# Three attention heads of a group transposed in one unit, their value products in the unit behind

## The chip, the cores and the metric

The kernel runs on one core of a Trainium2 chip. The metric is the device time of one execution in microseconds (us). Before the change it is 906.09 us, the median of three runs that lie between 906.04 and 906.09 us.

The engines of the core are named as in the profile. PE is TensorE, which multiplies matrices and writes its results to PSUM; PEld is its loading of weights, which runs beside the multiplying. DVE is VectorE, ACT is ScalarE, POOL is GpSimd, and SP issues most of the transfers. Each engine works through its own list of instructions in order, and an instruction can wait until another engine has counted up to a given number of instructions.

## The reference

One layer of an encoder, for 256 tokens of width 2048, all in fp32. What matters here is the attention group: 12 query heads of 128 columns share 4 heads of keys and values, so that three query heads belong to one group of keys.

```python
h = _rmsnorm(x, norm1_g)
proj = h @ w_in                      # q | k | v | u
scores = jnp.einsum('bnqkgd,bnskd->bnkgqs', qb, kb) * (HEAD_DIM ** -0.5) + alibi
p = jnp.exp(scores - m)
p = p / (jnp.sum(p, axis=-1, keepdims=True) + jnp.exp(sink_b - m))
out = jnp.einsum('bnkgqs,bnskd->bnqkgd', p.astype(v.dtype), vb)
f = jnp.real(jnp.fft.fft2(ug, axes=(1, 3), norm='ortho'))   # then a linear map per group
a, f = _rmsnorm(attention, attn_out_g), _rmsnorm(fourier, fourier_out_g)
x = x + jnp.concatenate([a, f], axis=-1) @ w_out
x = x + _conv_ffn(_rmsnorm(x, norm2_g), w_up, dw_w, dw_b, w_down)
```

A final RMSNorm follows. The attention and the Fourier group are each normed over their own width, so the kernel needs a sum of squares per token for each of the two.

## The kernel before

Weights come from memory in pieces of 1 MB. ACT and DVE split each piece into a high and a low part (`parts`, lines 185 and 186), and PE multiplies with both parts. The work of PE on one piece is a *unit*. Units 8 to 23 compute the projections of 4 key heads and 12 query heads, in the order k, q, q, q for each group; head 0 is unit 9, head 1 unit 10, head 2 unit 11, head 3 unit 13, and so on up to head 11 in unit 23. Units 24 to 39 are the output projection, and the feed-forward part follows.

A unit of a projection is 16 pairs of matmuls, one of 128x512 with the high part (line 394) and one of 128x256 with the low part (line 396). The attention work of the heads is laid between the units, by a table of what is done how many units after the unit of a head: the scores (line 662) two units later, the exponentials behind them (line 692), the division by the sum (`weigh`, line 705) three units later, the transposing of the weights on PE four units later (`turn`, four 128x128 transposes, line 712, read out by `turn_out`: ACT writes the high part `pt0`, line 724, DVE the low part `pt1`, line 725), the product with the values five units later (`values`, six matmuls, line 734, read out by `values_out`: ACT squares, line 491, and writes the high part of `cat`, line 234, DVE its low part, line 235). The squares of each head are added up by POOL (line 496) into `sq_a`. `total` (line 503) sums them over the partitions with matmuls that have a column of ones.

Each unit `i` runs in four steps, which fix the order of each engine's list: the list `before` (PE work of the heads), then the unit's own matmuls, then `beside` (reading out on ACT and DVE), then the split of the weights for unit `i + 2`, then `behind`.

```python
    def unit(i, work):
        run(before, i)
        work(*halves.pop(i))
        run(beside, i)
        step(i)
        run(behind, i)
```

The buffers that matter are eight PSUM banks, four in the pool `mm` (the projections, `ps_k` and `ps_q`, and most value products, `ps_o`) and four in `dn` (scores `ps_s`, transposes `ps_t`, sums `ps_totf` and `ps_tota`, the last value products), three buffers for `parts`, and four for `sc`, the attention weights. A new tile takes a buffer that has come free; where none is free its first writer waits for the reader that gives one up. The tile that collects a head's squares (`sq1`) has one buffer.

Of the kernel before, what the change touches and what calls it, by code (L numbers as in the profile page):

```python
# [9 lines left out]
F32R = mybir.dt.float32r  # L10
# [3 lines left out]
P = 128  # L14
# [6 lines left out]
GQA = 3  # L21
NG = 4
AW = NH * HD
FW = NG * P
# [27 lines left out]
N_OUT = N_QK + len(QK_ORDER)  # L52
# [44 lines left out]
def block_kernel(  # L97
# [24 lines left out]
    mm = ctx.enter_context(tc.tile_pool(name="mm", bufs=4, space=bass.MemoryType.PSUM))  # L122
    dn = ctx.enter_context(tc.tile_pool(name="dn", bufs=4, space=bass.MemoryType.PSUM))

    def f32(ap):
        return ap.bitcast(F32)
# [182 lines left out]
    ph = pa.enter_context(tc.tile_pool(name="pa", bufs=1))  # L309
# [103 lines left out]
    before, beside, behind = {}, {}, {}  # L413

    def at(when, i, f, *a):
        when.setdefault(i, []).append((f, a))
# [190 lines left out]
    def fourier_channels_steps():  # L607
        for g in range(NG):
            i = 9 + g
            at(beside, i, fourier_channels_copy, g)  # L610
            at(beside, i + 1, fourier_channels_join, g)
            at(behind, i + 1, fourier_channels_out, g)
        at(beside, 15, total_scale, "f", FW)


    ps_v = [bank(mm, f"ps_v{b}") for b in range(2)]
# [15 lines left out]
    def qk_out(kind, h, ps):  # L632
        tmp = ph.tile([P, S], F32, tag="tmp", name=f"tmp_{kind}{h}", bufs=2)
        nc.scalar.activation(tmp, ps[:, S : 2 * S], AF.Copy)
        add = ph.tile([P, S], F32, tag="add", name=f"add_{kind}{h}", bufs=2)
        nc.vector.tensor_tensor(add, ps[:, 0:S], tmp, ALU.add)
        if kind == "k":
            nc.vector.tensor_tensor(add, add, r1b, ALU.mult)
        st["add", kind, h] = add
# [77 lines left out]

    def turn_out(h):
        ps = st.pop(("t", h))
        pt = [  # L720
            ph.tile([P, 512], F32R, tag=f"pt{q}", name=f"pt{q}{h}", bufs=2)
            for q in range(2)
        ]
        nc.scalar.activation(pt[0], ps, AF.Copy)
        nc.vector.tensor_tensor(pt[1], ps, f32(pt[0]), ALU.subtract)
        st["p", h] = pt
# [20 lines left out]
    slot_of = {kh: N_QK + n for n, kh in enumerate(QK_ORDER)}  # L747
    for i in range(N_QK, N_OUT + 8):
        heads = {i - s: h for (kind, h), s in slot_of.items() if kind == "q"}
        new = [kh for kh, s in slot_of.items() if i - s == 1]  # L750
        if i - 9 in range(NG):
            at(before, i, fourier_channels, i - 9)
        if 5 in heads:
            at(before, i, values, heads[5], mm if i < N_OUT else dn)
        if 4 in heads:
            at(before, i, turn, heads[4])
        if i == 15:
            at(before, i, total, sq_f, "f")
        if 2 in heads:
            at(before, i, scores, heads[2])  # L760

        for kind, h in new:
            if kind == "q":
                at(beside, i, lambda k=kind, h=h: qk_out(k, h, st.pop(("ps", k, h))))
        if 4 in heads:
            at(beside, i, turn_out, heads[4])
        if 3 in heads:
            at(beside, i, weigh, heads[3])
        for kind, h in new:
            if kind == "k":  # L770
                at(beside, i, lambda k=kind, h=h: qk_out(k, h, st.pop(("ps", k, h))))
            at(beside, i, qk_parts, kind, h)
        if 2 in heads:
            at(beside, i, scores_out, heads[2])
            at(behind, i, exps, heads[2])
        if 5 in heads:
            at(beside, i, values_out, heads[5])

    fourier_channels_steps()
    for n, (kind, h) in enumerate(QK_ORDER):  # L780

# [56 lines left out]
    for n, (c, kq) in enumerate(OUT_ORDER):  # L838
        i = N_OUT + n
# [391 lines left out]
    i = up_index[n]  # L1231
# [156 lines left out]
```

## Time and profile before

| what | value |
|---|---|
| median of three runs | 906.09 us |
| the profiled execution: its own time | 906.14 us |
| span from first to last instruction | 904.4 us |
| granted TensorE clock, mean | 0.998 |
| PE, matmuls | 895.6 us busy, 99% |
| PEld, weight loads | 811.1 us, 90% |
| DVE | 745.1 us, 82% |
| ACT | 547.2 us, 61% |
| POOL | 51.7 us, 6% |

The profile comes from one execution, and its sums are made against that execution: its time of 906.14 us is 1.74 us more than its span, and 0.05 us above the median. A timeline row gives start and length of an instruction, or of some in a run (x4), then engine, line, output<-inputs; in brackets stands how long the engine stood idle before it and for whom. The stated length of a matmul holds its passage through the array, so matmuls overlap in the rows: what a matmul costs is read from start to start. The stretch that the change touches lies between 80 and 190 us of the span.

### The profile page before, as it was taken

The numbers are of one execution on the slowest core, as the hardware profiler recorded it, in microseconds if no ns is written. First come the engines' busy times: TensorE is split into PE (matmuls) and PEld (weight loads), VectorE is DVE, ScalarE is ACT, GpSimd is POOL, SyncE is SP. The second block draws the span as 40 slices with busy tenths as digits, with TensorE's granted clock in tenths as the row PEclk, the third lists the DMA queues.
The fourth block names the chain that finished last, engine by engine and source line by source line (L and its number), as shares of the span: only waits on it lengthen the run. The fifth ranks groups of instructions, "written<-read, shape, count | busy, mean of one in ns | idle before, by whom it ended". The sixth has DMA issues, their size and how long they took to land.

```text
span 904.4 us, 12754 instructions
## 1 busy us (share of the span) xinstructions
PE 895.6 (99%) x5073; PEld 811.1 (90%) x5073; DVE 745.1 (82%) x892; ACT 547.2 (61%) x663; POOL 51.7 (6%) x65
## 2 busy tenths in 40 slices
PE   9999999999999999999999999999999999999996
PEld 8899999888899999999999999999999999999885
DVE  7579888666668877889887998878988789998996
ACT  7767677555454656556565565566655566656544
POOL 0001111000000000000000000000000000000004
PEclk9999999999999999999999999999999999999999
DMA  9864544456568678677898779887787988779652
GB/s 365 332 234 145 187 152 175 146 180 226 192 231 283 231 242 251 188 257 230 275 266 271 245 258 287 258 276 237 275 250 245 312 263 262 242 240 286 217 196 94
DMA packets 32908, 214.86 MB, mean 238 GB/s; under 512 B 3632, under 2 KB 4016, under 8 KB 8528
## 3 DMA queue, kind: packets, MB, share of 16 engines
q1 hardware_dynamic: 28448, 183.89, 54.5%
q0 software_dynamic: 4112, 29.49, 17.1%
q8 instruction: 40, 0.66, 0.3%
q10 hardware_dynamic: 288, 0.66, 0.2%
q14 instruction: 20, 0.16, 0.0%
HBM read 211.93 MB, written 2.10 MB: 237 GB/s over the span
## 4 chain that ended last, share of the span: by engine, by line
PE 95%; DVE 2%; POOL 1%; issue 1%; ACT 0%; POOLq 0%; ACTq 0%; DVEq 0%
PE ps_val L394 17%; PE ps_gate L394 17%; PE ps_gate L396 8%; PE ps_val L396 8%; PE ps_q L394 5%; PE ps_P L1105 3%; PE ps_P L1107 3%; PE ps_P L1106 3%; PE ps_N L1105 2%; PE ps_N L1107 2%; PE ps_N L1106 2%; PE ps_u L286 2%; PE ps_q L396 2%; PE ps_a L377 2%; PE ps_a L379 2%; PE ps_a L378 2%
## 5 line engine op out<-in xcount | busy, mean ns | idle before, releaser
L186 DVE TENSOR_TENSOR parts<-raw,parts 128x2048 fp32r<-128x2048 f32 (+1 forms) x129 | 293.2, 2273 | 49.4 <-ACT parts L185 48.9
L185 ACT ACTIVATE parts<-raw 128x2048 fp32r<-128x2048 f32 (+1 forms) x129 | 245.4, 1902 | 46.7 <-PE ps_a L379 12.4
L394 PE MATMUL ps_val<-hU,parts 128*128 128x512 f32 x688 | 227.7, 382 | 0.0
L394 PE MATMUL ps_gate<-hU,parts 128*128 128x512 f32 x688 | 227.3, 382 | 0.0
L396 PE MATMUL ps_val<-hU,parts 128*128 128x256 f32 x688 | 187.5, 273 | 0.0
L396 PE MATMUL ps_gate<-hU,parts 128*128 128x256 f32 x688 | 186.9, 273 | 0.0
L394 PEld LDWEIGHTS ps_val<-hU,parts 128*128 128x128 f32 x688 | 130.0, 189 | 18.1
L394 PEld LDWEIGHTS ps_gate<-hU,parts 128*128 128x128 f32 x688 | 130.0, 189 | 18.1
L396 PEld LDWEIGHTS ps_val<-hU,parts 128*128 128x128 f32 x688 | 132.0, 192 | 0.8
L396 PEld LDWEIGHTS ps_gate<-hU,parts 128*128 128x128 f32 x688 | 131.8, 192 | 0.9
L883 ACT ACTIVATE ft_g<-ps_gate 128x256 f32<-128x256 f32 x43 | 16.5, 384 | 112.7 <-PE ps_gate L396 110.0
L394 PE MATMUL ps_q<-hT,parts 128*128 128x512 f32 x192 | 62.6, 384 | 0.0
L883 ACT ACTIVATE ft_v<-ps_val 128x256 f32<-128x256 f32 x43 | 16.5, 384 | 73.4 <-PE ps_val L396 73.4
L1105 PE MATMUL ps_P<-parts_P,op_P 128*128 128x512 f32 x144 | 54.7, 380 | 0.0
L1106 PE MATMUL ps_P<-parts_P,op_P 128*128 128x512 f32 x144 | 54.6, 379 | 0.0
L1107 PE MATMUL ps_P<-parts_P,op_P 128*128 128x512 f32 x144 | 54.6, 379 | 0.0
L396 PE MATMUL ps_q<-hT,parts 128*128 128x256 f32 x192 | 50.4, 273 | 0.0
L991 DVE TENSOR_TENSOR parts_N<-sumw,parts_N 128x2048 fp32r<-128x2048 f32 x18 | 41.2, 2289 | 9.9 <-ACT parts_N L990 9.9
L1105 PE MATMUL ps_N<-parts_N,op_N 128*128 128x512 f32 x108 | 41.0, 380 | 0.0
L1106 PE MATMUL ps_N<-parts_N,op_N 128*128 128x512 f32 x108 | 40.9, 379 | 0.0
L1107 PE MATMUL ps_N<-parts_N,op_N 128*128 128x512 f32 x108 | 40.9, 379 | 0.0
L394 PEld LDWEIGHTS ps_q<-hT,parts 128*128 128x128 f32 x192 | 36.1, 189 | 4.7
(346 smaller groups left out, 1557.7 us busy)
## 6 DMA issues: line engine op xcount, KB each, us to landing
raw<-in_w_up SPq DMA_DIRECT2D x86, 1024.0 KB, 6.2
raw<-in_w_in SPq DMA_DIRECT2D x20, 1024.0 KB, 5.0
sumw<-in_w_down POOLq DMA_DIRECT2D x18, 1024.0 KB, 8.5
raw<-in_w_out SPq DMA_DIRECT2D x16, 1024.0 KB, 4.8
raw<-in_w_down_late SPq DMA_DIRECT2D x4, 1024.0 KB, 5.8
u_raw<-in_u_in SPq DMA_DIRECT2D x4, 768.0 KB, 9.3
raw<-in_w_down_last SPq DMA_DIRECT2D x4, 768.0 KB, 4.2
u_raw<-in_u_in SPq DMA_DIRECT2D x6, 384.0 KB, 6.3
```

The costliest lines, as they stand in the source:

```text
L185: nc.scalar.activation(hi, raw, AF.Copy)
L186: nc.vector.tensor_tensor(lo, raw, f32(hi), ALU.subtract)
L286: nc.tensor.matmul(ps_u[b], block(hk(k), part, b, True), in_turn(w), start=k == 0 and n == 0, stop=k == NK - 1 and n == 2,)
L377: nc.tensor.matmul(ps, ah, wh, start=first and q == q0, stop=False)
L378: nc.tensor.matmul(ps, al, wh, start=False, stop=False)
L394: nc.tensor.matmul(ps, hi[:, s], in_turn(h), start=k == 0, stop=False)
L396: nc.tensor.matmul(ps[:, 0:S], lo[:, s], in_turn(h)[:, 0:P], start=False, stop=k == NK - 1)
L883: nc.scalar.activation(tmp, ps[:, S : 2 * S], AF.Copy)
L991: nc.vector.tensor_tensor(lo, src, f32(hi), ALU.subtract)
L1105: nc.tensor.matmul(ps, o[:, 0, p, :], wh, start=first and p == 0, stop=False)
L1106: nc.tensor.matmul(ps, o[:, 1, p, :], wh, start=False, stop=False)
L1107: nc.tensor.matmul(ps, o[:, 0, p, :], wl, start=False, stop=end)
```

## The change

The transposes of the three heads of a group move together into one unit, four units after the last of the three; the first head's transposes move by two units and the second's by one. The three value products follow together in the next unit. The value product of the middle head takes its PSUM bank from `dn`, the two others from `mm`; from unit 24 on all are in `dn`, as before. `pt0` has three buffers in place of two. `pt1` has no buffers of its own any more and takes one of the four `sc` buffers. The sum over partitions of the Fourier squares, and what follows from it, move from unit 15 to unit 19. No arithmetic changes, and every instruction of before is there.

```diff
@@ fourier_channels_steps
-        at(beside, 15, total_scale, "f", FW)
+        at(beside, 19, total_scale, "f", FW)
@@ turn_out
         pt = [
-            ph.tile([P, 512], F32R, tag=f"pt{q}", name=f"pt{q}{h}", bufs=2)
-            for q in range(2)
+            ph.tile([P, 512], F32R, tag=tag, name=f"pt{q}{h}", bufs=bufs)
+            for q, (tag, bufs) in enumerate([("pt0", 3), ("sc", 4)])
         ]
@@ the loop over units that fills the lists
         heads = {i - s: h for (kind, h), s in slot_of.items() if kind == "q"}
+        turned, valued = (
+            range(h - GQA + 1, h + 1) if (h := heads.get(late, 0)) % GQA == GQA - 1 else ()
+            for late in (4, 5)
+        )
...
-        if 5 in heads:
-            at(before, i, values, heads[5], mm if i < N_OUT else dn)
-        if 4 in heads:
-            at(before, i, turn, heads[4])
-        if i == 15:
+        for h in valued:
+            at(before, i, values, h, dn if i >= N_OUT or h % GQA == 1 else mm)
+        for h in turned:
+            at(before, i, turn, h)
+        if i == 19:
             at(before, i, total, sq_f, "f")
...
-        if 4 in heads:
-            at(beside, i, turn_out, heads[4])
+        for h in turned:
+            at(beside, i, turn_out, h)
...
-        if 5 in heads:
-            at(beside, i, values_out, heads[5])
+        for h in valued:
+            at(beside, i, values_out, h)
```

The order of the engines' lists shows it at three places. A name is the tile with its number: `ps_t5` are the transposes of head 5, `ps_s6` the scores of head 6, `ps_o4` the value product of head 4; the number behind the last underscore is only a running count.

On PE, at the head of unit 19, which is the projection of head 8, before the change: the value product of head 4, the transposes of head 5, the scores of head 6.

```order
L734 MATMUL ps_o4_1330<-pt04_1308,v_hi_328 128x256
L734 MATMUL ps_o4_1330<-pt14_1309,v_hi_328 128x256
L734 MATMUL ps_o4_1330<-pt04_1308,v_lo_329 128x256
L734 MATMUL ps_o4_1330<-pt04_1308,v_hi_328 128x256
L734 MATMUL ps_o4_1330<-pt14_1309,v_hi_328 128x256
L734 MATMUL ps_o4_1330<-pt04_1308,v_lo_329 128x256
L712 MATMUL ps_t5_1337<-ident_110,sc5_1242 128x128 x4
L662 MATMUL ps_s6_1342<-kT2_1239,qT6_1316 128x256 x6
L394 MATMUL ps_q8_1349<-hT0_124,parts19_1249 128x512
```

The same place after the change, with the engines that an instruction waits for in brackets.

```order
L712 MATMUL ps_t3_1292<-ident_110,sc3_1052 128x128 x4
L712 MATMUL ps_t4_1297<-ident_110,sc4_1141 128x128 [waits DVE_49] x2
L712 MATMUL ps_t4_1297<-ident_110,sc4_1141 128x128 x2
L712 MATMUL ps_t5_1302<-ident_110,sc5_1226 128x128 [waits DVE_49,PE_49]
L712 MATMUL ps_t5_1302<-ident_110,sc5_1226 128x128 [waits DVE_49]
L712 MATMUL ps_t5_1302<-ident_110,sc5_1226 128x128 x2
L503 MATMUL ps_totf_1307<-ones_106,sq_f_331 128x1 [waits Pool_49]
L503 MATMUL ps_totf_1307<-ones_106,sq_f_331 128x1
L662 MATMUL ps_s6_1310<-kT2_1223,qT6_1284 128x256 [waits DVE_49]
L662 MATMUL ps_s6_1310<-kT2_1223,qT6_1284 128x256 x5
L394 MATMUL ps_q8_1317<-hT0_124,parts19_1233 128x512
```

Twelve transposes and the Fourier sum now stand ahead of the scores of head 6. That makes five tiles of `dn` in a row with four banks: `ps_s6` gets the bank of `ps_t3`, and its first matmul waits for the count of DVE that the subtraction of `pt13` reaches, the second reader of `ps_t3`.

On DVE, units 18 and 19 before the change, from the sum of head 6's projection on.

```order
L636 TENSOR_TENSOR add_q6_1306<-ps_q6_1193,tmp_q6_1304 128x256
L725 TENSOR_TENSOR pt14_1309<-ps_t4_1266,pt04_1308 128x512
L701 TENSOR_TENSOR sm5_1254<-sm5_1254,ex5_1255 128x2
L702 RECIPROCAL ex5_1255<-sm5_1254 128x2
L705 TENSOR_SCALAR sc5_1242<-sc5_1242,ex5_1255 128x256 x2
L235 TENSOR_SCALAR qT6_1316<-add_q6_1306,qT6_1316 128x256
L235 TENSOR_SCALAR cat3_1321<-ps_o3_1259,vec_87,cat3_1321 128x256
L186 TENSOR_TENSOR parts20_1325<-raw20_1093,parts20_1325 128x2048
L636 TENSOR_TENSOR add_q7_1384<-ps_q7_1271,tmp_q7_1382 128x256
L725 TENSOR_TENSOR pt15_1387<-ps_t5_1337,pt05_1386 128x512
```

The same place after the change; lines from 725 on stand one lower in the file, so 726 is the 725 of before.

```order
L636 TENSOR_TENSOR add_q6_1278<-ps_q6_1181,tmp_q6_1276 128x256
L701 TENSOR_TENSOR sm5_1238<-sm5_1238,ex5_1239 128x2
L702 RECIPROCAL ex5_1239<-sm5_1238 128x2
L705 TENSOR_SCALAR sc5_1226<-sc5_1226,ex5_1239 128x256 x2
L235 TENSOR_SCALAR qT6_1284<-add_q6_1278,qT6_1284 128x256
L186 TENSOR_TENSOR parts20_1287<-raw20_1062,parts20_1287 128x2048
L636 TENSOR_TENSOR add_q7_1352<-ps_q7_1243,tmp_q7_1350 128x256
L726 TENSOR_TENSOR pt13_1355<-ps_t3_1292,pt03_1354 128x512
L726 TENSOR_TENSOR pt14_1359<-ps_t4_1297,pt04_1358 128x512
L726 TENSOR_TENSOR pt15_1363<-ps_t5_1302,pt05_1362 128x512
L235 TENSOR_SCALAR qT7_1366<-add_q7_1352,qT7_1366 128x256
```

Unit 18 has lost the reading of a transpose and of a value product, and unit 19 has three readings of transposes in place of one.

On ACT, unit 16 before the change, from the copy of head 5's projection to the split.

```order
L634 ACTIVATE tmp_q5_1147<-ps_q5_1029 128x256
L234 ACTIVATE qT5_1155<-add_q5_1149 128x256
L491 ACTIVATE sq2_1165<-ps_o2_1100 128x256
L234 ACTIVATE cat2_1167<-ps_o2_1100,vec_87 128x256
L185 ACTIVATE parts18_1171<-raw18_925 128x2048
```

The same place after the change.

```order
L634 ACTIVATE tmp_q5_1130<-ps_q5_1000 128x256
L234 ACTIVATE qT5_1138<-add_q5_1132 128x256
L491 ACTIVATE sq_a_523<-ps_o0_1069 128x256
L234 ACTIVATE cat0_1149<-ps_o0_1069,vec_87 128x256
L491 ACTIVATE sq1_1152<-ps_o1_1076 128x256
L234 ACTIVATE cat1_1154<-ps_o1_1076,vec_87 128x256
L491 ACTIVATE sq2_1158<-ps_o2_1083 128x256
L234 ACTIVATE cat2_1160<-ps_o2_1083,vec_87 128x256
L185 ACTIVATE parts18_1164<-raw18_916 128x2048
```

All three value products are read out ahead of the split of the weights for unit 18, and the square of head 2 must wait until POOL has added that of head 1, since both use the one `sq1` buffer.

## The prediction

> **What bounds the kernel now.** I read the page first, then the table of the stretch from 50 to 200 us, which holds all the work that is moved, and then what PE waited for.
>
> ```profile
> PE 895.6 (99%) x5073; PEld 811.1 (90%) x5073; DVE 745.1 (82%) x892; ACT 547.2 (61%) x663; POOL 51.7 (6%) x65
> PE 95%; DVE 2%; POOL 1%; issue 1%; ACT 0%; POOLq 0%; ACTq 0%; DVEq 0%
> ```
>
> ```profile
> 50.00:200.00 150.00, 150.00 (x928) 137.86 (x927) 118.25 (x236) 98.49 (x176) 13.90 (x16) 1.00 0.51 179
> ```
>
> ```profile
> PE ps_warm L229 <- POOL ones L221: 1.0, 1, 1.0
> ```
>
> The second row of the page is the chain that ended last: 95% of it is PE. In the second fence the columns are the stretch, its length and the busy time of PE, PEld, DVE, ACT and POOL, then the granted clock (1.00). PE is busy for 150.00 of 150.00 us. The third fence is PE's whole list of waits: one, of 1.0 us, at the very start. So in this stretch the time is the sum of PE's start-to-start steps. The other engines matter only where they would make PE wait, and the change can win only if PE's steps get shorter.
>
> **The change, part by part: the move itself.** PE keeps every instruction, so the question is whether a run of transposes costs something for being a run. The timeline has a run of four in unit 14, and one of eight in the output projection.
>
> ```profile
> 87.64 0.60 PE L712 MATMUL ps_t<-ident,sc 128*128 128x128 f32 x4
> 88.00 0.46 PE L394 MATMUL ps_q<-hT,parts 128*128 128x512 f32 x1
> 88.30 0.27 PE L396 MATMUL ps_q<-hT,parts 128*128 128x256 f32 x1
> 88.41 0.38 PE L394 MATMUL ps_q<-hT,parts 128*128 128x512 f32 x1
> 88.63 0.27 PE L396 MATMUL ps_q<-hT,parts 128*128 128x256 f32 x1
> ...
> 206.78 1.04 PE L819 MATMUL ps_x<-ident,xs 128*128 128x128 f32 x8
> 207.57 0.46 PE L377 MATMUL ps_a<-parts,cat 128*128 128x512 f32 x1
> 207.87 0.38 PE L378 MATMUL ps_a<-parts,cat 128*128 128x512 f32 x1
> 208.09 0.38 PE L379 MATMUL ps_a<-parts,cat 128*128 128x512 f32 x1
> ```
>
> The 128x512 matmul behind the four transposes takes 0.30 us to the next start (88.00 to 88.30), an ordinary one 0.22 (88.41 to 88.63). Taken alone, that is 0.08 us lost at the end of each run; twelve runs become four, and 8 x 0.08 = 0.65 us would be won. But the last transpose gave way early: four of them plus that matmul take 88.30 - 87.64 = 0.66 us, less 0.22 is 0.44, or 0.11 for each transpose. Eight of them take 207.87 - 206.78 - 0.22 = 0.87, again 0.11 each. Twice the short run is 0.88, so a boundary costs 0.01 us at most. I take 0 and keep -0.65 us as the lower end. The value products are ordinary matmuls in either place: 0.
>
> **The scores of head 6.** At the head of unit 19 five tiles of `dn` are asked for and there are four banks. The scores of head 6 wait for the DVE subtraction of `pt13`, the last reader of the first transposes. The unit before the change has the same sequence (transpose, ACT copy, DVE subtraction) on one head:
>
> ```profile
> 119.49 2.29 DVE L186 TENSOR_TENSOR parts<-raw,parts 128x2048 fp32r<-128x2048 f32 x1 [0.20 <-ACT parts L185]
> 120.06 0.39 PE L734 MATMUL ps_o<-pt,v_hi 128*128 128x256 f32 x2
> 120.32 0.38 ACT L634 ACTIVATE tmp_q<-ps_q 128x256 f32<-128x256 f32 x1 [0.86 <-PE ps_q L396]
> 120.73 0.60 PE L712 MATMUL ps_t<-ident,sc 128*128 128x128 f32 x4
> 121.36 0.60 ACT L724 ACTIVATE pt<-ps_t 128x512 fp32r<-128x512 f32 x1 [0.66 <-PE ps_t L712]
> 121.70 0.42 DVE L636 TENSOR_TENSOR add_q<-ps_q,tmp_q 128x256 f32<-128x256 f32 x1
> 122.04 0.68 DVE L725 TENSOR_TENSOR pt<-ps_t,pt 128x512 fp32r<-128x512 f32 x1
> ```
>
> From the first transpose to the end of the subtraction: 122.04 + 0.68 - 120.73 = 1.99 us. ACT was idle before its copy and DVE took the subtraction as soon as the copy was there, so this is the shortest that the chain can be. What PE has to do meanwhile is the twelve transposes, 12 x 0.11 = 1.31 us, and the Fourier sum. The sum's price comes from unit 15, where it stands between transposes and scores:
>
> ```profile
> 93.99 0.60 PE L712 MATMUL ps_t<-ident,sc 128*128 128x128 f32 x4
> ...
> 95.54 0.38 PE L394 MATMUL ps_q<-hT,parts 128*128 128x512 f32 x1
> ...
> 101.45 0.83 PE L662 MATMUL ps_s<-kT,qT 128*128 128x256 f32 x6
> 102.12 0.38 PE L394 MATMUL ps_k<-hT,parts 128*128 128x512 f32 x1
> ```
>
> The six score matmuls alone take 102.12 - 101.45 = 0.67 us, so the sum takes 95.54 - 93.99 - 0.44 - 0.67 = 0.44. PE thus comes to the scores 1.31 + 0.44 = 1.75 us after the first transpose and waits 1.99 - 1.75 = 0.24 us. What starting again costs shows where PE before waits for a late DVE result by a hair:
>
> ```profile
> 194.13 1.40 DVE L796 SCALAR_TENSOR_TENSOR xs<-ps_a,rstda,xs 128x512 f32<-128x512 f32 x2
> 195.41 1.18 PE L819 MATMUL ps_x<-ident,xs 128*128 128x128 f32 x8
> 196.64 0.38 PE L378 MATMUL ps_a<-parts,cat 128*128 128x512 f32 x1
> ```
>
> Here eight transposes and one matmul take 1.23 us instead of 1.09. I take 0.1 us of that 0.14 for the restart: +0.34 us together.
>
> This holds if DVE has reached the subtraction in time. In unit 19 before, DVE began the unit's first work (the sum `add_q`, at 121.70) 1.64 us after the unit's first matmul (120.06), held by the split that began at 119.49. Unit 18 loses one subtraction and one `cat` on DVE, about 0.61 and 0.41 us, so the lag comes to 1.64 - 1.02 = 0.62; `add_q` is over before ACT's copy (0.63 + 0.60 us after the start), and the 1.99 us stand. With the full 1.64 the wait would be 1.64 + 0.34 + 0.68 - 1.75 + 0.1 = 1.01. Other units begin later:
>
> ```profile
> 86.97 0.39 PE L734 MATMUL ps_o<-pt,v_hi 128*128 128x256 f32 x2
> 91.02 0.41 DVE L636 TENSOR_TENSOR add_q<-ps_q,tmp_q 128x256 f32<-128x256 f32 x1
> ...
> 113.71 0.39 PE L734 MATMUL ps_o<-pt,v_hi 128*128 128x256 f32 x2
> 116.05 0.41 DVE L636 TENSOR_TENSOR add_q<-ps_q,tmp_q 128x256 f32<-128x256 f32 x1
> ```
>
> Unit 18 has a lag of 2.34 us and unit 14 one of 4.05, where the Fourier work of DVE also lies. With 2.34 the wait would be 1.71 us, which I keep as the upper end; with 4.05 it would be 3.42. I take the short chain, because unit 19 is nearest to its own row, and that row gets lighter.
>
> **The other pieces, which I cost at nothing.** Unit 16 reads out three value products in place of one, with the split of unit 18's weights behind them. The rows of one read-out, its split, POOL's sum of squares, and the one case in unit 28:
>
> ```profile
> 116.92 0.37 ACT L491 ACTIVATE sq<-ps_o 128x256 f32<-128x256 f32 x1
> 117.54 1.92 ACT L185 ACTIVATE parts<-raw 128x2048 fp32r<-128x2048 f32 x1
> ...
> 129.01 0.98 POOL L496 TENSOR_TENSOR sq_a<-sq_a,sq 128x256 f32<-128x256 f32 x1 [5.21 <-ACT sq L491]
> ...
> 178.75 0.39 PE L734 MATMUL ps_o<-pt,v_hi 128*128 128x256 f32 x2
> 180.46 0.48 DVE L235 SCALAR_TENSOR_TENSOR cat<-ps_o,vec,cat 128x256 fp32r<-128x256 f32 x1 [1.27 <-ACT cat L234]
> raw<-in_w_in SPq DMA_DIRECT2D x20, 1024.0 KB, 5.0
> ```
>
> A read-out takes ACT 117.54 - 116.92 = 0.62 us. Since the `sq1` buffer is single, the second and third square after the first that goes through it wait for POOL, at most 0.98 - 0.35 = 0.6 us each. Behind the waiting square stand the split and, behind it, DVE; two more read-outs and the waits make the split at most 2 x 0.62 + 2 x 0.6 = 2.4 us later. A unit takes at least 16 x 0.33 = 5.2 us (88.30 to 88.63 is one pair), and the split serves the unit after next, so its cover is more than 5 us; without it the 2.4 us would show in each of four groups. Each split also lets SP issue the load of a piece that is used three units later, 15 us; 2.4 us late, it still lands in 5.0 us (last row). In unit 28 five tiles of `dn` come up again, and the fifth, half of the Fourier product, waits for the read-out of head 9. One such read-out was over 180.46 + 0.48 - 178.75 = 2.2 us after its product began; ahead of the waiting matmul stand three products (3 x 0.67) and 12 matmuls of 0.22, or 4.6 us. `pt1` in the `sc` buffers waits for tiles whose last reader ran one unit earlier or more. The Fourier sum four units later is used in unit 29, some 60 us on.
>
> **Sum.** 906.14 us (span 904.4) + 0 for the move + 0.34 for the wait = 906.48 for the profiled execution, which stands 0.05 above the median: 906.4.
>
> [...] The row first: behind the run of eight transposes the matmul steps are 0.22 us at once (207.87 to 208.09), and the granted clock of the stretch is 1.00. [...] The trace before shows no run over 0.87 us, so it doesn't decide on 1.31.
>
> **The rivals.**
> - *DVE is late in unit 19* (slower than before). The place is the wait of the scores of head 6. It costs lag + 0.34 + 0.68 - 1.75 + 0.1, so it decides from a lag of 2.4 us on; with unit 14's 4.05 it gives 906.09 + 3.42 = 909.5. For it: unit 16 carries two read-outs more, and lags of 2.3 and 4.1 us exist. Against: units 17 and 18 both lose a subtraction. Chance 8%.
> - *The runs lose PE's clock.* The first six 128x512 matmuls of the kernel show what slow steps look like:
>
> ```profile
> 4.57 2.35 PE L286 MATMUL ps_u<-parts,hT 128*128 128x512 f32 x6
> 6.75 0.33 PE L301 MATMUL ps_warm<-ones 128*128 128x64 f32 x2
> ```
>
>   They take (6.75 - 4.57) / 6 = 0.36 us against 0.22. If PE worked at that rate for as long as each run (1.31 us) in four groups, 4 x 1.31 x 0.64 = 3.4 us, or 909.5. Against it: the run of eight. [...] Chance 2%.
> - *Fewer boundaries win*: -0.65 + 0.34 = -0.31, or 905.8; without any wait 905.4. For it the 0.30 us step, against it the sums of 0.44 and 0.87. Chance 5%.
> - *The change does nothing*: the wait is hidden, 906.1. It needs a chain 0.24 us shorter than the shortest row. Chance 8%.
>
> **How the numbers follow.** A measurement of this kernel tells about 0.2%, or 1.8 us, from no change. The forecast, a short wait in unit 19 alone, has 74%; it and the two small cases before this paragraph stay within 1.8 us: 87%, of which I give 2 away. Slower by more than 0.2% are the late DVE and the clock, 10%, and 2% more for a wait that I overlook: 12%. Faster by more needs PE steps that shrink, for which no row speaks: 3%. The range runs from the boundary gain without a wait (905.4) to the wait at unit 18's lag (906.09 + 1.71 = 907.8).
>
> **What would show it.** In the changed profile PE's list of waits should have one new row, the scores (662) waiting for the subtraction of `pt1`, once and for 0.2 to 0.5 us. The twelve transposes should take 0.11 us each and the matmul behind them 0.22, at clock 1.00. The prediction is wrong if PE waits at other units, if the wait of head 6 exceeds 1.8 us, or if matmul steps in the touched units differ from 0.22 and 0.11.

## The result and the profile after

The changed kernel takes 909.75 us, the median of six runs between 908.08 and 910.39, beside 906.09 us for the kernel before (905.99 to 906.19, six runs). The ratio is 1.0035, with a 95% interval of 1.0025 to 1.0045: slower by about 3.7 us, where 906.4 was forecast and the range ended at 907.8. The six times lie in two groups: 908.08 twice, and 909.58 to 910.39 four times. The profiled execution is of the second group, 909.94 us with a span of 908.2.

The page of the changed kernel, PE's whole list of waits, and the chain that ended last:

```profile
PE 897.6 (99%) x5073; PEld 812.8 (89%) x5073; DVE 743.7 (82%) x892; ACT 548.2 (60%) x663; POOL 53.4 (6%) x65
...
PE 87%; DVE 7%; ACT 2%; issue 2%; POOL 1%; POOLq 0%; ACTq 0%; DVEq 0%
```

```profile
PE ps_s L662 <- DVE pt L726: 1.8, 1, 1.8
PE ps_warm L229 <- POOL ones L221: 1.0, 1, 1.0
```

PE has one new wait, the one that the prediction named: the scores of head 6 wait for DVE's subtraction of `pt13`. One wait of 1.8 us is enough to move 8% of the chain from PE to the other engines, since the chain is followed back from that wait through all the work that DVE and ACT had carried ahead of it.

PE in unit 15, where nothing waits, and at the head of unit 19, from the timeline of the changed kernel:

```profile
91.89 1.47 PE L712 MATMUL ps_t<-ident,sc 128*128 128x128 f32 x12
93.11 0.91 PE L662 MATMUL ps_s<-kT,qT 128*128 128x256 f32 x6
93.87 0.38 PE L394 MATMUL ps_q<-hT,parts 128*128 128x512 f32 x1
...
118.18 1.47 PE L712 MATMUL ps_t<-ident,sc 128*128 128x128 f32 x12
119.49 0.50 PE L503 MATMUL ps_totf<-ones,sq_f 128*128 128x1 f32 x4
121.84 0.94 PE L662 MATMUL ps_s<-kT,qT 128*128 128x256 f32 x6 [1.85 <-DVE pt L726]
122.61 0.38 PE L394 MATMUL ps_q<-hT,parts 128*128 128x512 f32 x1
122.83 0.28 PE L396 MATMUL ps_q<-hT,parts 128*128 128x256 f32 x1
122.94 0.60 PE L394 MATMUL ps_q<-hT,parts 128*128 128x512 f32 x1
123.33 0.42 PE L396 MATMUL ps_q<-hT,parts 128*128 128x256 f32 x1
```

In unit 15 twelve transposes and six scores take 93.87 - 91.89 = 1.98 us, which is 12 x 0.109 + 0.67: a run of twelve costs nothing beyond its members. In unit 19 the transposes start at 118.18 and take 1.31; the first experiment shows the Fourier sum at 0.37; so PE could have begun the scores at 119.86 and began at 121.84. The wait costs 1.98 us. From 122.94 on a pair of matmuls takes 0.64 us (0.43 between the later starts, and 0.21) in place of 0.33. The windows of 3.41 us around it (length, busy time of PE, PEld, DVE, ACT and POOL, granted clock, DMA share, GB/s):

```profile
116.13:119.55 3.42, 3.42 (x30) 3.29 (x28) 2.27 (x7) 3.35 (x5) 0.00 (x0) 1.00 0.79 268
119.55:122.96 3.41, 1.56 (x14) 1.45 (x14) 3.41 (x6) 2.58 (x4) 0.00 (x0) 1.00 0.42 106
122.96:126.37 3.41, 3.41 (x13) 2.96 (x12) 3.34 (x10) 1.96 (x6) 1.77 (x1) 0.50 0.59 245
126.37:129.78 3.41, 3.41 (x23) 3.14 (x23) 0.35 (x1) 0.00 (x1) 0.94 (x1) 1.00 0.60 180
```

PE was busy for 1.56 of the 3.41 us of the window with the wait. In the next window the clock is 0.50, and 13 matmuls run where 23 run in the window behind. At a clock of 0.50 that window loses half of its 3.41 us, or 1.7 us, an estimate from this row. With it the profiled execution adds up: 906.14 + 1.98 + 1.7 = 909.8, and 909.94 was measured. The two executions at 908.08 were not traced, but their mean clock of 0.998 (0.996 in the other four) and the sum 906.1 + 1.98 = 908.08 speak for no window at half clock in them.

Why DVE was late is read from the sums `add_k` and `add_q`, with which it takes up PE's results in units 17 and 19. First the rows of the kernel before, then those of the changed one:

```profile
105.82 2.29 DVE L186 TENSOR_TENSOR parts<-raw,parts 128x2048 fp32r<-128x2048 f32 x1 [0.25 <-ACT parts L185]
...
107.36 0.60 PE L712 MATMUL ps_t<-ident,sc 128*128 128x128 f32 x4
...
108.63 0.69 DVE L725 TENSOR_TENSOR pt<-ps_t,pt 128x512 fp32r<-128x512 f32 x1 [0.52 <-ACT pt L724]
...
110.16 0.41 DVE L636 TENSOR_TENSOR add_k<-ps_k,tmp_k 128x256 f32<-128x256 f32 x1
```

```profile
106.77 2.29 DVE L186 TENSOR_TENSOR parts<-raw,parts 128x2048 fp32r<-128x2048 f32 x1 [1.17 <-ACT parts L185]
107.03 0.83 PE L662 MATMUL ps_s<-kT,qT 128*128 128x256 f32 x6
...
109.89 0.42 DVE L636 TENSOR_TENSOR add_k<-ps_k,tmp_k 128x256 f32<-128x256 f32 x1
...
115.75 0.42 DVE L636 TENSOR_TENSOR add_q<-ps_q,tmp_q 128x256 f32<-128x256 f32 x1
...
116.62 1.90 ACT L185 ACTIVATE parts<-raw 128x2048 fp32r<-128x2048 f32 x1
...
118.56 2.29 DVE L186 TENSOR_TENSOR parts<-raw,parts 128x2048 fp32r<-128x2048 f32 x1 [1.08 <-ACT parts L185]
118.81 1.57 ACT L725 ACTIVATE pt<-ps_t 128x512 fp32r<-128x512 f32 x3
120.77 0.42 DVE L636 TENSOR_TENSOR add_q<-ps_q,tmp_q 128x256 f32<-128x256 f32 x1
121.10 1.88 DVE L726 TENSOR_TENSOR pt<-ps_t,pt 128x512 fp32r<-128x512 f32 x3
```

ACT had the copy of the first transposes under way at 118.81, but DVE was in the split of the weights until 120.77, 2.59 us after PE's unit had begun at 118.18. Before, that lag was 1.64 us. Unit 17 begins alike in both: a lag of 110.16 - 107.36 = 2.80 before, 109.89 - 107.03 = 2.86 after. Not that nothing changed ahead of it: PE has two more value products in unit 16, ACT and DVE have them to read out, so that DVE's split stands 1.17 us waiting for ACT in place of 0.25, and DVE is spared the subtraction of `pt13` (0.69 us, with 0.52 of waiting before it). These happen to balance. What makes the lag longer from there on lies between the two units. PE went from the start of unit 17 to that of unit 19 in 120.06 - 107.36 = 12.70 us before and in 118.18 - 107.03 = 11.15 after, because two runs of transposes (0.44 each) and one value product (0.67) have left these two units. DVE went from sum to sum in 121.70 - 110.16 = 11.54 before and in 120.77 - 109.89 = 10.88 after. PE gained 1.55 us, DVE only 0.66, and the lag grew by the difference: 1.64 + 1.55 - 0.66 + 0.06 = 2.59.

Why only 0.66? In unit 18 DVE is spared a subtraction (0.68 us) and a `cat` (some 0.4), but its split waits for ACT's half in both kernels, 0.20 us before and 1.08 us after. So ACT sets the pace there, and ACT is spared one read-out of a value product, 0.62 us: its half of the split starts 117.54 - 116.05 = 1.49 us after the sum of unit 18 before, and 116.62 - 115.75 = 0.87 us after. The way from `add_k` to the sum of unit 18 is the same in both (5.89 and 5.86 us).

### The profile page after: what moved, and what is told of

Read it like the earlier page. It is cut to its first block, busy times and chain, and to the rows that moved or that the text cites. A ratio compares the mean times of both kernels' runs of the same rounds, so it can differ in the third digit from the quotient of the medians.

```text
span 908.2 us, 12759 instructions
## 1 busy us (share of the span) xinstructions
PE 897.6 (99%) x5073; PEld 812.8 (89%) x5073; DVE 743.7 (82%) x892; ACT 548.2 (60%) x663; POOL 53.4 (6%) x65
## 4 chain that ended last, share of the span: by engine, by line
PE 87%; DVE 7%; ACT 2%; issue 2%; POOL 1%; POOLq 0%; ACTq 0%; DVEq 0%
PE ps_val L394 17%; PE ps_gate L394 17%; PE ps_val L396 8%; PE ps_gate L396 8%; PE ps_P L1111 3%; PE ps_P L1113 3%; PE ps_P L1112 3%; DVE parts L186 3%; PE ps_N L1111 2%; PE ps_N L1113 2%; PE ps_N L1112 2%; PE ps_u L286 2%; PE ps_a L377 2%; PE ps_a L378 2%; PE ps_a L379 2%
```

## The experiments

**One bank less asked for.** The Fourier sum takes its bank from the other pool, so that `ps_s6` finds a free one.

```diff
-        ps = bank(dn, "ps_tot" + part)
+        ps = bank(mm if part == "f" else dn, "ps_tot" + part)
```

> The changed kernel with one word altered: the Fourier sum of unit 19 takes its PSUM bank from `mm` instead of `dn`, so that four tiles of `dn` stand against four banks; PE's order is that of the changed kernel to the instruction. Theory (the whole loss is one wait for the fifth bank, and the half clock is the wait's work): no wait in unit 19, clock 1.00 throughout, 906.1 us, within 0.1 of before. Rival (runs of twelve transposes lower the clock, or bundling makes ACT and DVE late elsewhere): the half clock stays in some executions, 907.8, or waits appear in other units, over 906.5.

It takes 906.16 us (905.98 to 906.45, 11 runs) beside 906.13; the ratio is 1.0001 [0.9992, 1.0010]. Its timeline at unit 19:

```profile
117.90 1.47 PE L712 MATMUL ps_t<-ident,sc 128*128 128x128 f32 x12
119.21 0.50 PE L503 MATMUL ps_totf<-ones,sq_f 128*128 128x1 f32 x4
119.58 0.91 PE L662 MATMUL ps_s<-kT,qT 128*128 128x256 f32 x6
```

The scores follow the sum at once (119.58 - 119.21 = 0.37 us), the matmul steps behind them are the ordinary 0.22 us (120.33 to 120.55), and the mean clock of this execution is 0.997, within the 0.997 to 0.999 of the kernel before. DVE is as late here as in the changed kernel (`add_q` at 120.55, a lag of 2.65 us), and nothing waits for it. So the whole loss hangs on the fifth bank. Bundling the transposes and the products, the `pt1` tiles in the `sc` buffers and the three read-outs in one unit cost nothing that can be measured, and win nothing.

**The sum back in unit 15.** The changed kernel with the two numbers 19 set to 15 again.

```diff
-        at(beside, 19, total_scale, "f", FW)
+        at(beside, 15, total_scale, "f", FW)
...
-        if i == 19:
+        if i == 15:
```

> The bundling alone: the changed kernel with the Fourier sum back in unit 15, where it stood before. Now unit 15 asks for five tiles of `dn`. Theory of the fifth bank: the scores of head 3 wait for the subtraction of `pt10`. In the changed kernel's profile that subtraction ends near 96.6 us (start 95.91, two of them 1.28), and PE would come to the scores at 91.89 + 1.75 = 93.6, so the wait is about 2.9 us in unit 15 and none in unit 19: 909.0, or 910.7 where a window of half clock follows. Rival (the loss belongs to unit 19 and its order): 906.1.

It takes 911.08 us (910.78 to 911.50, four runs), ratio 1.0056 [1.0042, 1.0069]. PE's list of waits:

```profile
PE ps_s L662 <- DVE pt L726: 3.5, 1, 3.5
```

The wait has moved with the sum, into unit 15, where DVE is later than in unit 19, and unit 19 has none. DVE's lag there is 95.58 - 91.89 = 3.69 us in the trace of the changed kernel, from which 2.9 us of waiting were expected, and 96.02 - 91.74 = 4.28 in this one. A half-clock window follows here too, at 98.50, and the mean clock of the execution is 0.995. The late place of the sum makes the loss smaller, it doesn't cause it.

**The sum alone.** The kernel before, with only the sum moved.

```diff
-        at(beside, 15, total_scale, "f", FW)
+        at(beside, 19, total_scale, "f", FW)
...
-        if i == 15:
+        if i == 19:
```

> The other part of the change alone: the kernel before with only the Fourier sum and its scale moved from unit 15 to unit 19. Unit 19 then has three tiles of `dn`. Both theories: no wait, 906.1 us, within 0.1 of before. If the later sum itself costs something (on POOL, or for the output projection), it shows here.

906.24 us (906.08 to 906.47, 10 runs), ratio 1.0001 [0.9992, 1.0010], and no wait. The move of the sum loses nothing alone, and the bundling loses nothing where the sum takes its bank elsewhere: it takes three tiles of transposes and the sum in one unit and in one pool.

**The short chain.** The split of unit 20's weights, which holds DVE until 120.77, is moved behind the reading of the transposes in unit 19.

```diff
-        step(i)
+        if i == 19:
+            split(20)
+        if i != 18:
+            step(i)
```

> The changed kernel, but the split of the weights for unit 20 is moved from the end of unit 18 to unit 19, behind the reading of the three transposes, so that DVE is free when unit 19 begins. The fifth bank is still missing. Theory (the wait is long because DVE comes to the subtraction 2.6 us after the start of the unit): the wait shrinks to the shortest chain, 0.24 to 0.5 us, no half clock, 906.3 to 906.6. Rival (the chain of transpose, copy and subtraction is itself slow when three heads come together): a wait over 1 us remains, above 907.

906.56 us (906.33 to 907.18, 10 runs), ratio 1.0006 [0.9996, 1.0015]. PE's list of waits:

```profile
PE ps_s L665 <- DVE pt L729: 0.2, 1, 0.2
```

With DVE free, the wait is the short chain that the prediction had worked out (0.24 us, 0.34 with the restart; 0.43 by the medians). From the first transpose to the scores it takes 120.08 - 118.07 = 2.01 us, where 1.99 was worked out for the chain. The lateness of DVE is what made it 1.98.

**Were the three read-outs of unit 16 the cause of the lateness?** They are put behind the split of unit 18's weights.

```diff
-            at(beside, i, values_out, h)
+            at(behind if i == 16 else beside, i, values_out, h)
```

> The changed kernel, with one step turned round: in unit 16 the three value products of the first group are read out behind the split of unit 18's weights and the exponentials, not ahead of them. The fifth bank is still missing in unit 19. Theory (the three read-outs held up the split in unit 16, DVE stood 1.17 us for it there, and this lateness is carried to unit 19): DVE comes to the subtraction about 1.1 us sooner, the wait falls from 2.0 to about 0.9 us, too short for the clock, 907.0 to 907.2 us. Rival (the lateness comes from the chain of keys in unit 17 or from the split in unit 18): the wait stays near 2.0 us, 908.1, or 909.8 with a half window.

909.72 us (908.03 to 909.89, six runs), ratio 1.0036 [1.0023, 1.0049]: as the changed kernel, against the theory. The split does come earlier (104.20 in place of 106.77), but DVE's three `cat` then stand ahead of `add_k` in its place, and the last of them waits 0.74 us for ACT. In the rows of this run, `add_k` begins at 109.65 and `add_q` of unit 19 at 120.54, the same 10.89 us apart. That pointed to PE's side of the lag, which the next three runs test. It doesn't clear the read-outs: they stand ahead of `add_k` in either order.

**PE made to arrive later.** The first matmul of unit 18's projection is issued eight times, of unit 18's three times, or, as a control, of unit 20's eight times. Each repetition only overwrites the same values.

```diff
+                for _ in range(again[0] - 1 if k == 0 else 0):
+                    nc.tensor.matmul(ps, hi[:, s], in_turn(h), start=True, stop=True)
                 nc.tensor.matmul(ps, hi[:, s], in_turn(h), start=k == 0, stop=False)
...
         run(before, i)
+        again[0] = 8 if i == 18 else 1
         work(*halves.pop(i))
+        again[0] = 1
```

Eight times in unit 18:

> Theory: DVE was late in unit 19 because PE came early. From the start of unit 17 to that of unit 19 PE took 12.70 us before (107.36 to 120.06) and 11.15 after (107.03 to 118.18), 1.55 less, since two runs of transposes and one product went away; DVE's sums add_k/add_q of units 17 and 19 stood 11.54 us apart before (110.16 to 121.70) and 10.88 after (109.89 to 120.77), only 0.66 less. 1.64 + 1.55 - 0.66 + 0.07 (2.87 instead of 2.80 at the start of unit 17) = 2.60, and 2.59 was measured. So this kernel, which issues the first matmul of unit 18's projection eight times instead of once (7 x 0.22 = 1.54 us of added work, the same result), should have a lag of about 1.05 us and a wait of 0.44 us or less in unit 19, no half-clock window, and 906.1 + 1.54 + 0.44 = 908.1 us. Rival: something on DVE or ACT itself became later, for example the three read-outs of unit 16; then PE's arrival does not matter for where DVE stands... only if DVE is pushed too does the wait stay at 2.0, and the time is 909.6, or 911.4 with a half-clock window.

Three times in unit 18:

> As the kernel above with two repeated matmuls in unit 18 (0.44 us of added work). Theory: the wait of the scores of head 6 falls from 1.98 to 1.54 us, below the 1.79 us that never brought a half clock, so no execution has a half-clock window: 906.1 + 0.44 + 1.54 = 908.1 us in every execution, 1.6 less than the changed kernel's median although work is added. Rival (the length of the wait doesn't decide on the clock): the same share of half windows as before, and a median of 909.7 to 910.2.

Eight times in unit 20:

> Control: the seven repeated matmuls stand in unit 20, behind the wait. Theory: the wait of unit 19 stays at 1.98 us, the added 1.54 us are paid in full, and the half-clock window comes in most executions (with more matmuls behind it, it costs the same 1.7): 906.1 + 1.54 + 1.98 = 909.6, or 911.3 with the window. Rival (the added work takes the wait away wherever it stands): 908.1.

Measured are 908.37 us (908.01 to 908.98, 10 runs), 908.22 (908.10 to 910.21, eight runs) and 911.42 (910.14 to 911.72, four runs), beside 906.21 for the kernel before; the ratios are 1.0022 [1.0013, 1.0031], 1.0027 [1.0017, 1.0038] and 1.0053 [1.0038, 1.0068]. The timeline of the first of the three:

```profile
106.77 0.83 PE L668 MATMUL ps_s<-kT,qT 128*128 128x256 f32 x6
...
110.07 0.42 DVE L642 TENSOR_TENSOR add_k<-ps_k,tmp_k 128x256 f32<-128x256 f32 x1
...
119.43 1.47 PE L718 MATMUL ps_t<-ident,sc 128*128 128x128 f32 x12
120.95 0.42 DVE L642 TENSOR_TENSOR add_q<-ps_q,tmp_q 128x256 f32<-128x256 f32 x1
...
122.02 0.94 PE L668 MATMUL ps_s<-kT,qT 128*128 128x256 f32 x6 [0.77 <-DVE pt L732]
```

DVE's sums stand 120.95 - 110.07 = 10.88 us apart, to the hundredth as in the changed kernel, although PE now takes 119.43 - 106.77 = 12.66 us for the two units. So DVE goes at its own pace there, and the lag is the difference of two paces: 1.52 us, and a wait of 0.9. The forecast was a wait of 0.44 at most. In this execution DVE was late by 0.44 us more than in the changed kernel already at unit 17 (a lag of 3.30 against 2.86), which is the difference. The mean clock of all ten executions, 0.997 or 0.998, shows no half window, and 908.37 is 0.3 above the forecast. (One of the 17 executions of the kernel before in this series came in at 908.09, so a single time proves little.) The kernel with the sum back in unit 15 shows the two paces from the other side: DVE stands there 113.87 - 112.69 = 1.18 us behind PE in unit 17 and 124.74 - 123.84 = 0.90 in unit 19, since PE takes 11.15 us again and DVE 10.87.

The second run is the plainest: it does 0.44 us more work than the changed kernel and its median is 1.5 us shorter. Its wait is 1.5 us in the list, and six of eight executions are at 908.1 to 908.3; the other two, at 910.13 and 910.21, show a mean clock of 0.996, as the executions of the changed kernel with a half window do. The expectation had none. These two were not traced; if their wait is the 1.5 us of the traced one, such a wait doesn't rule the half window out. By the times it came less often in these few executions (two of eight, against four of six). The control has the same seven matmuls behind the wait; its rows:

```profile
121.88 0.97 PE L668 MATMUL ps_s<-kT,qT 128*128 128x256 f32 x6 [1.95 <-DVE pt L732]
122.66 0.64 PE L398 MATMUL ps_q<-hT,parts 128*128 128x512 f32 x1
123.08 0.42 PE L400 MATMUL ps_q<-hT,parts 128*128 128x256 f32 x1
```

The wait is as long as ever (1.95 us in the list), and the steps behind it are slow (122.66 to 123.08, 0.42 us in place of 0.22): 911.42, as expected of added work that is merely paid for.

**Do long runs of transposes lose the clock?** The first of these kernels, with every transpose issued six times over, so that runs of 72 stand on PE.

```diff
-                nc.tensor.transpose(
+                for _ in range(6):
+                    nc.tensor.transpose(
```

> The changed kernel with the Fourier sum's bank from `mm` (no wait), and every transpose issued six times in a row with the same result, so that each of the four groups has a run of 72 transposes, 72 x 0.109 = 7.9 us in place of 1.3; a window of 3.41 us lies wholly inside each run. Rival (transposes don't count as work for the clock): a window at 0.50 in or behind each run, four groups and about 1.7 us or more each: 906 + 26 + 7 = 939. Theory (only waiting lowers it): clock 1.00 in all of them, the runs at 0.109 us for each transpose, 906.1 + 4 x 6.55 = 932.3.

932.63 us in two runs. The run at unit 19 and the mean clock of the execution:

```profile
124.99 8.02 PE L713 MATMUL ps_t<-ident,sc 128*128 128x128 f32 x72
132.85 0.51 PE L503 MATMUL ps_totf<-ones,sq_f 128*128 128x1 f32 x4
```

```profile
core 0: 931.0 us, clock 0.999
```

72 transposes take 132.85 - 124.99 = 7.86 us, 0.109 each from the first to the last. The matmul step behind this run is the ordinary 0.22 us (133.97 to 134.19), and the mean clock of the execution, with four such runs in it, is 0.999, beside 0.997 to 0.999 in the kernel before. 7.9 us without any other matmul is over two windows of 3.41 us, so these runs of transposes did not lower the clock.

**Which waits halve the clock?** In the feed-forward part of the kernel before, 13 places make PE wait for copies that ACT takes from the bank just finished, one to six copies for waits of 0.7 to 3.8 us.

```diff
+            if n in ladder and items[n - 1][0] in ("gate", "val"):
+                dm = wp.tile([P, 512], F32, tag="junk", name=f"dm{n}")
+                for _ in range(ladder[n]):
+                    nc.scalar.activation(dm, was, AF.Copy)
+                nc.tensor.matmul(ps[:, 0:64], dm[:, 0:P], dm[:, 0:64], start=True, stop=True)
```

> The kernel before with thirteen waits of PE laid into the feed-forward part, far from any transposes. Ahead of an up-projection ACT copies the finished sum of the projection before it one to six times, and one small matmul (its result is overwritten) waits for the last copy. One copy of 128x512 takes ACT about 0.5 us, so the waits should be near 0.8, 1.3, 1.8, 2.3, 2.8 and 3.3 us for one to six copies, 40 copies and some 24 us in all. Theory (the wait alone lowers the clock, and one of 2.0 us is already enough where it lies well in a window of 3.41 us): the windows behind waits of 2.3 us and more have a granted clock of 0.50, some behind 1.8 as well, none behind 0.8 and 1.3; five to eight windows, about 906 + 24 + 9 to 14 = 939 to 944. Rival (in the changed kernel the twelve transposes were needed too, as they don't count as work): no half clock anywhere but perhaps behind 3.3 us, 930 to 932.

946.61 us in two runs, 2.6 above the expected range. Half clock begins at 304.81, 345.77, 431.10 and 676.86 us, and lasts one window, at 345.77 two, in the first of which PE waits again. All four starts lie whole multiples of 3.413 us apart, 12, 25 and 72 of them, on one grid through 372 us of work and waits. Two pairs of windows on that grid, the first around a wait of 1.94 us and the second around one of 2.57:

```profile
301.40:304.81 3.41, 1.47 (x10) 1.12 (x9) 0.65 (x2) 2.80 (x6) 0.00 (x0) 1.00 0.75 247
304.81:308.22 3.41, 3.41 (x13) 2.96 (x12) 2.64 (x3) 1.86 (x2) 0.00 (x0) 0.50 0.17 67
325.29:328.70 3.41, 1.62 (x10) 1.22 (x9) 1.77 (x2) 1.69 (x3) 0.88 (x1) 1.00 0.70 269
328.70:332.11 3.41, 2.63 (x17) 2.45 (x18) 1.42 (x3) 3.26 (x5) 0.00 (x0) 1.00 0.97 180
```

The shorter wait lies whole in one window (1.47 us busy), and the next window is at half clock. The longer one is cut by a boundary of the grid (1.79 and 0.78 us idle), and the clock stays full. A second wait of 1.94 us, cut into 1.56 and 0.38, stays without effect too. So the length of a wait doesn't tell these cases apart, and neither 1.94 us nor 2.57 us is enough by itself; where the grid cuts the wait does tell them apart. The last of these runs has two shorter waits at each of 13 places, about 1.3 and 1.2 us with some 1.1 us of matmuls between.

```diff
+                for _ in range(2):
+                    nc.scalar.activation(dm, was, AF.Copy)
+                nc.tensor.matmul(ps[:, 0:64], dm[:, 0:P], dm[:, 0:64], start=True, stop=True)
+                still_weights(hi, lo, ps, range(2))
+                for _ in range(3):
+                    nc.scalar.activation(dm, was, AF.Copy)
+                pd = bank(mm, f"ps_d{n}")
+                nc.tensor.matmul(pd[:, 0:64], dm[:, 0:P], dm[:, 0:64], start=True, stop=True)
+                still_weights(hi, lo, ps, range(2, NK))
```

> The kernel before with thirteen pairs of waits in the feed-forward part: a wait of PE of about 1.3 us (two copies on ACT), two steps of the projection (0.65 us of work), and a second wait of about 1.2 us (three more copies), so that a pair with its work takes 3.1 us. One of the two waits alone is shorter than every wait that lowered the clock so far (1.85 us and more within one window of 3.41 us). Theory (the clock goes by the sum of idle time within a window): windows that hold 1.85 us or more of a pair are followed by a window at 0.50, about half of the thirteen; 906 + 13 x 2.5 + 6 x 1.7 = 949. Rival (the length of one wait decides): clock 1.00 throughout, 906 + 33 = 939.

967.18 us (966.25 and 968.11), more than either side expected. Windows of it, in three groups:

```profile
286.30:289.71 3.41, 1.67 (x10) 1.05 (x8) 0.59 (x2) 2.25 (x4) 0.00 (x0) 1.00 0.89 180
289.71:293.13 3.42, 2.60 (x9) 2.33 (x10) 1.40 (x3) 3.29 (x5) 0.00 (x0) 0.50 0.98 316
293.13:296.54 3.41, 3.41 (x12) 2.96 (x12) 2.62 (x3) 0.00 (x0) 0.00 (x0) 0.50 0.41 120
...
388.70:392.11 3.41, 1.91 (x12) 1.27 (x10) 0.63 (x1) 2.02 (x4) 0.00 (x0) 1.00 0.94 344
392.11:395.53 3.42, 2.36 (x15) 2.21 (x16) 1.15 (x3) 3.39 (x5) 0.00 (x0) 1.00 0.40 170
...
569.60:573.02 3.42, 1.89 (x11) 1.55 (x12) 0.28 (x1) 2.83 (x7) 0.00 (x0) 1.00 1.01 426
573.02:576.43 3.41, 3.41 (x12) 2.88 (x11) 2.64 (x4) 3.10 (x4) 0.00 (x0) 0.50 0.15 62
```

The wait of 1.32 us and the first 0.42 us of the next one fall into the window from 286.30 (1.67 us busy), and the clock is halved behind it; where the grid leaves 1.91 us busy it isn't. The clock is halved at six places of this execution, each behind a window with parts of two waits, and behind none that held a single wait of 1.2 to 1.6 us. At three of them a second half window follows, as from 293.13, where the rest of the second wait falls into the first. In this run that speaks against the length of one wait, and for what comes together in a window. The idle time in the records doesn't order all cases, though: the window from 569.60 was idle for 1.52 us, in two parts, and lost the clock, while one that held a single wait of 1.62 us didn't.

The times of both expectations were too low, not because of the waits (33.5 us by PE's list, 32.5 expected) but because of what stands around them. The 26 small matmuls, at 0.24 us each, take 6 us. From start to start a wait costs 0.16 us more than the list has (1.48 us for a listed 1.32 at the one that ends at 569.89), and the 128x512 matmul behind it takes 0.30 us in place of 0.22; for 26 waits that is 6 again. The nine half windows take 14: 1.7 where PE was busy throughout, some 1.3 in the three where it waited again. That makes 60 us, and the span is 964.5 - 904.4 = 60.1 longer than before.

## Why the prediction was wrong

- *The place.* Right: one new wait on PE, the scores of head 6 for `pt13` in unit 19, and no other. The first experiment shows that the loss is this wait and its consequence, and nothing else.
- *The move itself at nothing.* Right: 0.109 us for each transpose in runs of 12, no gain and no loss at the boundaries (906.16 against 906.13 us without the wait).
- *The shortest chain, 0.34 us.* Right: 0.43 us when DVE is free. One of its terms is a little off, the Fourier sum, which takes 0.37 us and not 0.44.
- *"The lag comes to 1.64 - 1.02 = 0.62".* This is the step that failed. It took from the lag what DVE no longer has to do in unit 18, and left out that the same bundling takes work from PE. A lag is the difference between two engines, and PE lost more: 1.55 us of transposes and one product, between the starts of units 17 and 19. Of the 1.02 us on DVE only 0.66 came through, since its split waits for ACT's half, and that came sooner only by the one read-out that ACT is spared. 0.62 + 1.55 + (1.02 - 0.66) + 0.06 = 2.59, the lag measured. The 1.55 could have been had from rows that the prediction quotes (2 x 0.44 + 0.67). The lag would then have been 2.17 us and the wait, by the prediction's own formula, 1.5.
- *The rival "DVE is late in unit 19".* Its formula holds: 2.59 + 0.34 + 0.68 - 1.75 + 0.1 = 1.96 us, against 1.98 measured, and it gives 906.09 + 1.96 = 908.05 for the executions that came in at 908.08. The 8% were wrong. The reason against it, that units 17 and 18 lose a subtraction, was the reason for it: what leaves these units leaves PE too. Its reason for, the two read-outs more in unit 16, stays open. They do hold DVE ahead of `add_k`, by 0.92 us more waiting for ACT and 0.78 us for two more `cat`, but they hold PE too, by two products of 0.67. Putting the read-outs behind the split changed nothing, and no run took them away.
- *The clock.* The half-clock window, traced in one execution and told in three more by their time and their mean clock of 0.996, adds some 1.7 us in four of six and decides the median. The prediction had a lost clock only as a result of long runs of transposes, and runs of 72 left the mean clock at 0.999. It came behind the wait of 1.98 us; without that wait, in the first experiment, the mean clock of all 11 executions is 0.997 or 0.998.
- *The other pieces at nothing.* Right as far as the time goes: the kernel without the fifth bank, which has all of them, takes what the kernel before takes.
- *What would make it wrong.* Two of the three signs named came up: the wait of head 6 exceeds 1.8 us, and the matmul steps behind it are 0.43 and 0.21.

## What to carry to other kernels

When work is moved off a stretch, write down for each pair of engines how much both lose there; the lag of a reader follows the difference, and taking work from the bound engine makes a reader later beside it, unless the reader is spared as much. Work that an engine is spared counts only where it doesn't wait for another one behind it. Count the tiles that are asked for between two reads against the banks of their pool: a tile too many costs the chain from writer to reader (0.43 us here) where the reader is early, and the reader's lag on top where it isn't. A PE wait can have a second price: behind waits of 1.98 and 1.94 us, and behind one of 1.32 us with 0.42 us of the next in its window, a window of 3.41 us stood at clock 0.50, which costs some 1.7 us where PE is busy throughout; behind another wait of 1.94 us, and behind one of 2.57, none did.

## What the runs showed of the hardware

In these traces half clock came in windows of 3.41 us. In the changed kernel one window stood at 0.50 (122.96 to 126.37); in the ladder of waits the four starts lay 12, 25 and 72 times 3.413 us apart. Each of the half-clock windows shown above begins behind a window in which PE was idle for a part, or behind another one at half clock. By PE's records of these traces, 1.47 and 1.56 us busy of 3.41 brought it, 1.62 and 1.79 didn't, 1.67 and 1.89 did, and 1.91 didn't; so between 1.62 and 1.89 us the busy time in the records doesn't tell which windows bring it. Behind one window at half clock with 2.60 us busy (289.71) the next was at 0.50 too. Counted from the start of the span, the half-clock windows stand some 0.1 us behind a multiple of 3.413 in the changed kernel (122.96), 1.0 us in the ladder (304.81) and 3.0 us in the double waits (289.71), so the grid falls differently in the traced executions. By the times, the wait cost some 2.0 us in two executions of the changed kernel and 3.5 to 4.3 in four; that its place on the grid decided between them is an estimate from the two pairs of windows of the ladder, since only one of the six was traced.

What exactly counts as busy within a window stays open, and so does the pace of DVE in units 17 and 18 (10.9 us between its sums in all the runs with the bundled heads): that its split waits 1.1 us for ACT there is seen in the rows, but no run took that wait away, nor the read-outs of unit 16.
